# A two-layer decoder trunk: norm scales spread by two float32r products, and narrower scores for the first query blocks

## The chip, the cores and the metric

The kernel runs on one core of a Trainium2 chip. A core has TensorE (PE in the rows; its weight loads stand apart as PEld), VectorE (DVE), ScalarE (ACT), GpSimd (POOL) and the DMA queues, here all issued from SyncE (SP). The metric is device time in microseconds for one execution, the median of several runs; less is better.

## What is computed

The input is 512 tokens of 1024 features in float32. Two layers follow, each with a token mixer and a gated MLP; every sub-layer has an RMS norm ahead of it and is added to the residual, and a last norm ends the trunk. Layer 0 mixes tokens by causal means over windows of 2, 4, 8 and 16; layer 1 is attention with 16 heads on 4 key-value heads, over a sliding window of 128 keys, with a sink for each head and a linear bias over distance.

```python
def rms_norm(x, g):
    y = xf * lax.rsqrt(jnp.mean(xf * xf, axis=-1, keepdims=True) + RMS_EPS)
    return (y * g).astype(x.dtype)

# attention, for each block of 128 queries: the keys of its own and of the previous block
scores = jnp.einsum('bnqkgd,bnskd->bnkgqs', q, kb) * (HEAD_DIM ** -0.5)
mask = ((dist >= 0) & (dist < WINDOW))[None] & (key_pos >= 0)[:, None, :]
scores = jnp.where(mask, scores + bias, -jnp.inf)
p = jnp.exp(scores - m)
probs = p / (jnp.sum(p, axis=-1, keepdims=True) + jnp.exp(sink - m))
o = jnp.einsum('bnkgqs,bnskd->bnqkgd', probs, vb)

# MLP
u = h @ w_in                     # 1024 -> 2 x 2816
c = causal_depthwise_conv(u, width 3) + conv_b
h = h + (a * silu(g)) @ w_out    # a, g: the halves of c

for i in range(DEPTH):           # DEPTH = 2
    h = h + mixer_i(rms_norm(h, norm_mix[i]))
    h = h + conv_glu_ffn(rms_norm(h, norm_ffn[i]), ...)
return rms_norm(h, norm_f)
```

The first query block (b = 0) has no previous block, so only 128 of its 256 key columns are ever valid.

## The kernel before

Activations lie with features on the partitions: eight tiles `h` of 128 features by 512 tokens. Nearly all the work is matrix products. Every float32 operand of them is split into a high part in float32r (a rounding by an ACT copy, names ending in h) and the rest (a DVE or POOL subtraction, names ending in l), and `mm3` (L82 to L86) makes three products of them: high by high (L84), weight-high by low (L85), weight-low by high (L86). In the rows a product's operands stand as out<-moving,stationary or in the other order, and float32r tiles that PE reads are printed as f32. Weights come by `fetch` from SP's queue, three raw tiles deep, and are split by `weights` (L93 to L102).

PSUM has eight banks, handed out in rings by name. In the MLP six banks form the ring of the projections (`ps`), two the ring `aux`.

A norm (class `Norm`) is applied late. `stats` (L233 to L240) sums the squares over the features by products of `n_acc` with two columns of `ones`, and gives `n_r`, 128 tokens on the partitions by 4 token tiles. The scale is needed along the free dimension, the same on all partitions, so `spread` (L242 to L252) makes for each token tile the diagonal matrix `n_d` of the scales (DVE, L247) and multiplies it by the full matrix of ones in f32 (L248, two records in the trace for each product); ACT copies the bank to `n_rb` (L251). `spread` is called four times: in the first half of the MLP of layer 0 (two groups of products behind the statistics), in the attention (behind the query projection 2, and ahead of the products with `wv`), in the MLP of layer 1, and for the first 256 tokens at the end. In the MLP the products of the first groups run before the scale is known: four banks wait for `n_rb`, which the first step of the conv (L365) multiplies them with.

In the attention there are 16 units (n, b), a group n of four heads that share keys by a block b of 128 queries. For a unit, `scores` (L593 to L630) makes eight products (L609) of 256 moving columns, a high and a low part of the keys for each of four heads; a query tile `q` holds a head in one half of the partitions and the rest of its splitting in the other. DVE adds the bias and finds the largest (L612), ACT takes the exponential (L625), POOL divides (L629). For b = 0 these read 128 columns only: `w` is 128 there and 256 elsewhere. `transposed` turns the result on PE (L637), ACT and DVE split it (`th` L640, `tl` L641), and `weighted` multiplies it by the values; ACT and DVE split that into `oh` and `ol` (L656, L657). The steps of units 4, 2 and 0 places back are put together, and pieces of the query projections (`fill_q`) and of the output projection (`fill_wo`) are put between them at a fixed rate, so that PE has work while the other engines do the softmax. `queries` makes a new query tile from a bank: DVE scales (L513), ACT rounds (L520), DVE subtracts (L521), for two tiles.

The code gives each engine's instructions in program order, and a scheduler of the tile framework, which has its own durations for each instruction, moves them before the program is built, except for those held by `pin`. So a change in one place moves instructions in others.

Of the kernel before, what the change touches and what calls it, by code (L numbers as in the profile page):

```python
# [19 lines left out]
F32 = mybir.dt.float32  # L20
F32R = mybir.dt.float32r
I32 = mybir.dt.int32
AF = mybir.ActivationFunctionType
ALU = mybir.AluOpType
AX = mybir.AxisListType

P = 128
D = 1024
S = 512
# [28 lines left out]
def trunk(ctx: ExitStack, tc: tile.TileContext, x_tok, x_t, vecs, w_pool, w_kq, w_v, w_o, w_in, w_out, out_a, out_b):  # L58
    nc = tc.nc
    V, A, G, T = nc.vector, nc.scalar, nc.gpsimd, nc.tensor  # L60
    PSUM = bass.MemoryType.PSUM

    cst = ctx.enter_context(tc.tile_pool(name="cst", bufs=1))
    wp = ctx.enter_context(tc.tile_pool(name="wp", bufs=4))
    xp = ctx.enter_context(tc.tile_pool(name="xp", bufs=NC))
    sm = ctx.enter_context(tc.tile_pool(name="sm", bufs=2))


    def small(pool, n, words, dt=F32, **kw):
        return pool.tile([P, words], dt, **kw)[:, :n]  # L70
# [6 lines left out]
    def bank(tag):  # L77
        rings[tag].append(rings[tag].pop(0))
        return banks[rings[tag][-1]]
# [77 lines left out]
    ident = cst.tile([P, P], F32, name="ident")  # L157
# [11 lines left out]
    for g, w in enumerate(WINDOWS):  # L169
# [5 lines left out]
        f = band[:, 4 + g, : w - 1]  # L175
# [3 lines left out]
            edge_copy(g)  # L179
    ones = cst.tile([P, P], F32, name="ones")  # L180
    G.memset(ones, 1.0)


    def rsqrt_mean(dst, ssq, n, root=False):
# [28 lines left out]
    class Norm:  # L213
# [27 lines left out]

        def spread(self, ps, r, tiles=range(NT)):  # L242

            dg = sm.tile([P, S], F32, tag="sq", name=f"{self.name}_d")
            for i, j in enumerate(tiles):
                sl = slice(j * P, (j + 1) * P)
                V.tensor_scalar(dg[:, sl], ident, r[:, i : i + 1], None, ALU.mult)  # L247
                T.matmul(ps[:, sl], lhsT=ones, rhs=dg[:, sl], start=True, stop=True)  # L248
            rb = sm.tile([P, S], F32, tag="rb", name=f"{self.name}_rb", bufs=1)
            lo, hi = tiles[0] * P, (tiles[-1] + 1) * P  # L250
            A.activation(rb[:, lo:hi], ps[:, lo:hi], AF.Copy)  # L251
            return rb  # L252

# [183 lines left out]
    with tc.tile_pool(name="ap", bufs=2) as ap:  # L437
# [40 lines left out]
        r = norm1.stats(bank("av"))  # L478
# [51 lines left out]
        for j in range(NT):  # L530
            ps = vps[j // 2][:, (j % 2) * 256 : (j % 2 + 1) * 256]
            vv = ap.tile([P, 256], F32, tag="vv", name=f"vv{j}", bufs=1)
            V.scalar_tensor_tensor(vv, ps, r[:, j : j + 1], vec[:, V_BV : V_BV + 256], ALU.mult, ALU.add)
            dh, dl = (t[:, j, : 8 * HD].rearrange("p (n z d) -> p n z d", n=4, z=2)[:, :, 1, :] for t in (vh, vl))
# [58 lines left out]
        def scores(n, b):  # L593
            w = P if b == 0 else 2 * P
            neg = small(ap, 4, 32, tag="neg", name=f"neg{n}{b}", bufs=3)
            den = small(ap, 4, 16, tag="den", name=f"den{n}{b}", bufs=3)
            sink = nsink[:, 4 * n : 4 * n + 4]
            kk = max(b - 1, 0) * P
            sc = []
            for pr in range(2):  # L600
                ps = bank("s")

                st = ap.tile([P, 2, 2 * P + 32], F32, tag="sc", name=f"sc{n}{b}{pr}", bufs=6)
                G.tensor_copy(st[:, :, w], sink[:, 2 * pr : 2 * pr + 2])
                for par in range(2):
                    o = ps[:, par * 256 : par * 256 + 256]
                    qt = q[2 * n + pr][par][:, b * P : (b + 1) * P]
                    for x, kt in enumerate(key[n]):
                        T.matmul(o, lhsT=qt, rhs=kt[:, kk : kk + 256], start=x == 0, stop=x == 1)  # L609
                for par in range(2):  # L610
                    i = 2 * pr + par
                    V.tensor_tensor_reduce(  # L612
                        out=st[:, par, :w],
                        in0=ps[:, par * 256 : par * 256 + w],
                        in1=dist[:, 2 * P - w :],
                        scale=-slopes[4 * n + i],
                        scalar=sink[:, i : i + 1],
                        op0=ALU.add,
                        op1=ALU.min,
                        accum_out=neg[:, i : i + 1],  # L620
                    )
                sc.append(st)
            for i in range(4):
                t = sc[i // 2][:, i % 2, : w + 1]
                A.activation(t, t, AF.Exp, bias=neg[:, i : i + 1], scale=-1.0, accum_out=den[:, i : i + 1])  # L625
            V.reciprocal(den, den)
            for i in range(4):
                t = sc[i // 2][:, i % 2, :w]
                G.tensor_scalar(t, t, den[:, i : i + 1], 1.0, ALU.mult, ALU.mult)  # L629
            return sc  # L630
# [32 lines left out]
        for i in range(NU + 4):  # L663
            base = AHEAD + i * RATE
            have = max(i - 4, 0)
            if i < NU:
                n, b = units[i]
                if b == 0:
                    fill(2 * n * NC, 0)
                sc[i] = scores(n, b)  # L670
                if b == 2 and n + 1 < NKV:
                    key[n + 1] = keys(n + 1)
            fill(base + 2 * RATE / 3, have)
            if 0 <= i - 4 < NU:
                weighted(*units[i - 4], pt.pop(i - 4))
            if 0 <= i - 2 < NU:
                pt[i - 2] = transposed(*units[i - 2], sc.pop(i - 2))
            fill(base + RATE, have)
# [11 lines left out]
    with tc.tile_pool(name="fp1", bufs=2) as fp:  # L690
# [33 lines left out]
        w = {m: (kept_weights if m == NB else out_weights)(1, 1, m) for m in range(NB, NC)}  # L724
# [5 lines left out]
        for m in range(NB, NC):  # L730
# [3 lines left out]
            elif m == NB + 1:  # L734
                rb = norm3.spread(bank("aux"), ra, range(2))
                turn(NB)
                for c in range(NC):
                    o = fp.tile([P, HS], F32, tag="o", name=f"o{c}", bufs=4)
# [5 lines left out]
        sq = norm3.square(NC - 1, HS, S)  # L744
        scale_chunk(NC - 1, HS, S)
        ps = bank("aux")
        for x, t in enumerate((norm3.acc, sq)):
            for j in range(2):
                T.matmul(
                    ps[:, 2 * j : 2 * j + 2],  # L750
                    lhsT=t[:, HS + j * P : HS + (j + 1) * P],
                    rhs=ones[:, :2],
                    start=x == 0 and j == 0,
                    stop=x == 1,
# [3 lines left out]
        r = small(sm, NT, 32, tag="r", name="n3b_r")  # L758
        for j in range(2):
            rsqrt_mean(r[:, j : j + 1], ps[:, 2 * j : 2 * j + 1], 1, root=True)  # L760
        for j in range(2):
            for a in range(2):
                o = fp.tile([P, S], F32, tag="ob", name=f"ob{j}{a}", bufs=4)
# [67 lines left out]
```

## Time and profile before

| | us |
|---|---|
| median of 3 runs | 924.77 |
| lowest and highest | 924.59, 926.54 |
| the profiled execution | 924.49 |
| its span, first to last instruction | 922.8 |
| PE busy, products | 912.7 |
| DVE busy | 574.1 |
| ACT busy | 421.2 |
| POOL busy | 128.8 |

Rows below come from the profiled execution, whose times start at the span's beginning. A row of the timeline has the start, the time from the start to the end of the row, the engine, the line, the operation, out<-in, the shape, and how many alike are put together; brackets hold how long the engine stood idle before and what ended it. The granted clock of PE is at its upper level in all of the span (mean 0.999).

### The profile page before, as it was taken

What the parts mean: (1) busy time and instruction counts of PE and PEld (TensorE: products, weight loads), DVE (VectorE), ACT (ScalarE), POOL (GpSimd) and SP (SyncE); (2) the same over time, 40 slices, a digit from 0 to 9 for tenths busy, and PEclk for the clock granted to TensorE, in tenths of its full rate; (3) what the DMA queues carried; (4) which work ended last, traced back from release to release, by engine and by line L of the source; (5) the groups of instructions that cost most, each with busy time, mean ns of one, the idle gap of its engine ahead of it and who ended that gap; (6) DMA issues with size and microseconds to landing.
All of it is one profiled execution on the core that took longest, in us unless ns stands there. A gap on an engine that the chain in (4) does not pass through costs nothing.

```text
span 922.8 us, 11710 instructions
## 1 busy us (share of the span) xinstructions
PE 912.7 (99%) x4419; PEld 769.1 (83%) x4419; DVE 574.1 (62%) x958; ACT 421.2 (46%) x666; POOL 128.8 (14%) x232
## 2 busy tenths in 40 slices
PE   8999999999999999999999999999999999999997
PEld 7888888888888888898888888888888888888896
DVE  7589766335777654455787472987743377677423
ACT  7654443223444443436887441644422244444532
POOL 3800000000000001226665040000000000000022
PEclk9999999999999999999999999999999999999999
DMA  8233322333223223322110041142233423222312
GB/s 334 70 114 114 110 68 80 94 129 114 92 92 101 70 80 101 129 92 92 47 47 24 27 137 68 67 160 85 65 93 100 137 91 101 105 77 64 95 61 92
DMA packets 28855, 88.13 MB, mean 96 GB/s; under 512 B 3200, under 2 KB 4352, under 8 KB 28800
## 3 DMA queue, kind: packets, MB, share of 16 engines
q1 hardware_dynamic: 28800, 87.40, 28.9%
q8 instruction: 34, 0.56, 0.2%
q14 instruction: 21, 0.17, 0.1%
HBM read 85.29 MB, written 2.10 MB: 95 GB/s over the span
## 4 chain that ended last, share of the span: by engine, by line
PE 91%; POOL 2%; issue 2%; ACT 1%; DMA 1%; DVE 1%; SPq 0%; ACTq 0%; POOLq 0%; DVEq 0%
PE bank L84 29%; PE bank L85 29%; PE bank L86 29%; POOL wi_l L101 2%; PE bank L609 1%; DMA wi_raw<-w_in 1%; PE bank L637 1%; POOL n_acc L231 1%; ACT sc L625 1%; PE bank L248 0%; DVE wi_l L101 0%; PE bank L237 0%; ACT q L520 0%; ACT wo_h L98 0%; SPq L145 0%
## 5 line engine op out<-in xcount | busy, mean ns | idle before, releaser
L98 ACT ACTIVATE wi_h<-wi_raw 128x1024 fp32r<-128x1024 f32 x88 | 93.2, 1062 | 102.2 <-PE bank L85 97.7
L84 PE MATMUL bank<-f0x_h,wi_h 128*128 128x512 f32 x352 | 137.1, 390 | 0.0
L84 PE MATMUL bank<-f1x_h,wi_h 128*128 128x512 f32 x352 | 137.1, 390 | 0.0
L84 PE MATMUL bank<-zh,wo_h 128*128 128x512 f32 (+1 forms) x363 | 137.1, 378 | 0.0
L86 PE MATMUL bank<-f0x_h,wi_l 128*128 128x512 f32 x352 | 137.0, 389 | 0.0
L86 PE MATMUL bank<-f1x_h,wi_l 128*128 128x512 f32 x352 | 136.9, 389 | 0.0
L85 PE MATMUL bank<-f1x_l,wi_h 128*128 128x512 f32 x352 | 136.9, 389 | 0.0
L85 PE MATMUL bank<-f0x_l,wi_h 128*128 128x512 f32 x352 | 136.9, 389 | 0.0
L86 PE MATMUL bank<-zh,wo_l 128*128 128x512 f32 (+1 forms) x363 | 136.6, 376 | 0.0
L85 PE MATMUL bank<-zl,wo_h 128*128 128x512 f32 (+1 forms) x363 | 136.5, 376 | 0.0
L231 POOL TENSOR_TENSOR n_acc<-n_acc,n_sq 128x512 f32<-128x512 f32 (+1 forms) x28 | 37.2, 1328 | 708.6 <-ACT n_sq L222 701.8
L101 DVE TENSOR_TENSOR wi_l<-wi_raw,wi_h 128x1024 fp32r<-128x1024 f32 x84 | 103.6, 1236 | 50.0 <-ACT wi_h L98 48.0
L98 ACT ACTIVATE wo_h<-wo_raw 128x768 fp32r<-128x768 f32 (+1 forms) x70 | 57.6, 824 | 124.0 <-PE bank L85 112.0
L365 DVE TENSOR_TENSOR c_u<-bank,n_rb 128x512 f32<-128x512 f32 x88 | 60.0, 687 | 76.3 <-PE bank L86 76.3
L101 DVE TENSOR_TENSOR wo_l<-wo_raw,wo_h 128x768 fp32r<-128x768 f32 (+1 forms) x66 | 60.4, 915 | 54.5 <-ACT wo_h L98 54.3
L86 PEld LDWEIGHTS bank<-zh,wo_l 128*128 128x128 f32 x363 | 68.3, 188 | 12.5
L85 PEld LDWEIGHTS bank<-zl,wo_h 128*128 128x128 f32 x363 | 68.3, 188 | 12.4
L84 PEld LDWEIGHTS bank<-zh,wo_h 128*128 128x128 f32 x363 | 68.3, 188 | 12.3
L86 PEld LDWEIGHTS bank<-f0x_h,wi_l 128*128 128x128 f32 x352 | 66.1, 188 | 13.8
L86 PEld LDWEIGHTS bank<-f1x_h,wi_l 128*128 128x128 f32 x352 | 66.1, 188 | 13.8
L84 PEld LDWEIGHTS bank<-f1x_h,wi_h 128*128 128x128 f32 x352 | 66.1, 188 | 13.7
L84 PEld LDWEIGHTS bank<-f0x_h,wi_h 128*128 128x128 f32 x352 | 66.1, 188 | 13.7
(173 smaller groups left out, 1471.3 us busy)
## 6 DMA issues: line engine op xcount, KB each, us to landing
wi_raw<-w_in SPq DMA_DIRECT2D x88, 512.0 KB, 3.2
wo_raw<-w_out SPq DMA_DIRECT2D x31, 384.0 KB, 3.0
wo_raw<-w_out SPq DMA_DIRECT2D x31, 320.0 KB, 2.9
kq_raw<-w_kq SPq DMA_DIRECT2D x10, 512.0 KB, 3.2
wo_raw<-w_o SPq DMA_DIRECT2D x8, 512.0 KB, 3.2
xt<-x_tok SPq DMA_DIRECT2D x4, 512.0 KB, 5.1
h<-x_t SPq DMA_DIRECT2D x8, 256.0 KB, 8.4
wpool_raw<-w_pool SPq DMA_DIRECT2D x2, 512.0 KB, 7.9
```

What stands on the lines that cost most here:

```text
L84: T.matmul(ps, lhsT=wh, rhs=xh, start=start, stop=False, **kw)
L85: T.matmul(ps, lhsT=wh, rhs=xl, start=False, stop=False, **kw)
L86: T.matmul(ps, lhsT=wl, rhs=xh, start=False, stop=stop, **kw)
L98: pin(A.activation(h[:, :n], raw[:, :n], AF.Copy))
L101: (eng or V).tensor_tensor(l[:, o], raw[:, o], h[:, o].bitcast(F32), ALU.subtract)
L231: eng.tensor_tensor(self.acc[:, lo:hi], self.acc[:, lo:hi], sq[:, lo:hi], ALU.add)
L365: V.tensor_tensor(u, ps, rb, ALU.mult)
L609: T.matmul(o, lhsT=qt, rhs=kt[:, kk : kk + 256], start=x == 0, stop=x == 1)
L625: A.activation(t, t, AF.Exp, bias=neg[:, i : i + 1], scale=-1.0, accum_out=den[:, i : i + 1])
L637: T.transpose(ps[:, i * P : (i + 1) * P], sc[i // 2][:, i % 2, kb * P : (kb + 1) * P], ident)
```

## The change

`spread` makes two diagonals for each token tile, a rounded one in float32r on ACT (`n_dh`) and the rest on DVE (`n_dl`), and then multiplies all token tiles at once: one product of 512 columns with each diagonal tile, 256 columns in the last call, against a float32r copy of the ones, accumulated in the bank. In `scores` the moving side has `w` columns, so 128 for b = 0 and 256 for the others as before; 32 of the 128 products are narrower.

```diff
     G.memset(ones, 1.0)
+    ones_r = cst.tile([P, P], F32R, name="ones_r")
+    G.tensor_copy(ones_r, ones)
...
         def spread(self, ps, r, tiles=range(NT)):
-            dg = sm.tile([P, S], F32, tag="sq", name=f"{self.name}_d")
+            dh, dl = (sm.tile([P, S], F32R, tag="sq", name=f"{self.name}_d{x}") for x in "hl")
+            lo, hi = tiles[0] * P, (tiles[-1] + 1) * P
             for i, j in enumerate(tiles):
                 sl = slice(j * P, (j + 1) * P)
-                V.tensor_scalar(dg[:, sl], ident, r[:, i : i + 1], None, ALU.mult)
-                T.matmul(ps[:, sl], lhsT=ones, rhs=dg[:, sl], start=True, stop=True)
+                A.activation(dh[:, sl], ident, AF.Copy, scale=r[:, i : i + 1])
+                V.scalar_tensor_tensor(dl[:, sl], ident, r[:, i : i + 1], dh[:, sl].bitcast(F32), ALU.mult, ALU.subtract)
+            for x, d in enumerate((dh, dl)):
+                T.matmul(ps[:, lo:hi], lhsT=ones_r, rhs=d[:, lo:hi], start=x == 0, stop=x == 1)
             rb = sm.tile([P, S], F32, tag="rb", name=f"{self.name}_rb", bufs=1)
-            lo, hi = tiles[0] * P, (tiles[-1] + 1) * P
             A.activation(rb[:, lo:hi], ps[:, lo:hi], AF.Copy)
...
-                    o = ps[:, par * 256 : par * 256 + 256]
+                    o = ps[:, par * 256 : par * 256 + w]
...
-                        T.matmul(o, lhsT=qt, rhs=kt[:, kk : kk + 256], start=x == 0, stop=x == 1)
+                        T.matmul(o, lhsT=qt, rhs=kt[:, kk : kk + w], start=x == 0, stop=x == 1)
```

Lines after the change are two higher behind L181 and four higher behind L248. The scheduler moves instructions in three places that the prediction speaks of.

PE in the first half of the MLP of layer 0, where the scales are spread, the change with - and + (`wi_2_0` is the weight group behind the spread; a product that stands there four times is two records each in the trace):

```order
 L86 MATMUL bank_70<-f0x_h,wi_2_1_l 128x512
-L248 MATMUL bank_77<-n_d,ones 128x128 x4
 L84 MATMUL bank_71<-f0x_h,wi_2_0_h 128x512
+L253 MATMUL bank_77<-n_dh,ones_r 128x512
+L253 MATMUL bank_77<-n_dl,ones_r 128x512
 L85 MATMUL bank_71<-f0x_l,wi_2_0_h 128x512
```

The two new products have moved behind one product of the next group. In the attention the first of them stands behind the first product of `wv` and the second behind its second; in layer 1 the first stands behind one product of the next group and the second behind four more.

ACT in the attention, units of group 2 (`sc` and `neg` are the scores and the largest of them, `q_0` a query tile of the last group), before:

```order
L98 ACTIVATE wo_h<-wo_raw 128x1024
L625 ACTIVATE sc_3964,den_3963<-sc_3964,neg_3962 128x257 x2
L625 ACTIVATE sc_3972,den_3963<-sc_3972,neg_3962 128x257 x2
L520 ACTIVATE q_0_3993<-bank_75,bqs 64x512
L656 ACTIVATE oh<-bank_71 128x2x128
L640 ACTIVATE th_4020<-bank_76 128x512
```

The same place after:

```order
L629 ACTIVATE sc_3972,den_3971<-sc_3972,neg_3970 128x257 x2
L629 ACTIVATE sc_3980,den_3971<-sc_3980,neg_3970 128x257 x2
L98 ACTIVATE wo_h<-wo_raw 128x1024
L524 ACTIVATE q_0_4001<-bank_75,bqs 64x512
L660 ACTIVATE oh<-bank_71 128x2x128
L644 ACTIVATE th_4028<-bank_76 128x512
```

The splitting of an output weight has moved from ahead of the four exponentials to behind them, and ahead of the query tile, `oh` and `th`.

PE at the first unit of head group 3 (`q7_0` is half of the last query tile, `wo0` the first output weight), before:

```order
L609 MATMUL bank2_72<-kh3_4062,q6_1_3996 128x256
L609 MATMUL bank2_72<-kl3_4063,q6_1_3996 128x256
L84 MATMUL bank5_75<-oh_3361,wo0_h_4201 128x512
L85 MATMUL bank5_75<-ol_3362,wo0_h_4201 128x512
L86 MATMUL bank5_75<-oh_3361,wo0_l_4202 128x512
L84 MATMUL bank5_75<-oh_3361,wo0_h_4201 128x512
L85 MATMUL bank5_75<-ol_3362,wo0_h_4201 128x512
L86 MATMUL bank5_75<-oh_3361,wo0_l_4202 128x512
L609 MATMUL bank3_73<-kh3_4062,q7_0_4136 128x256
L609 MATMUL bank3_73<-kl3_4063,q7_0_4136 128x256
```

The same place after:

```order
L613 MATMUL bank2_72<-kh3_4070,q6_1_4004 128x128
L613 MATMUL bank2_72<-kl3_4071,q6_1_4004 128x128
L84 MATMUL bank5_75<-oh_3369,wo0_h_4209 128x512
L85 MATMUL bank5_75<-ol_3370,wo0_h_4209 128x512
L86 MATMUL bank5_75<-oh_3369,wo0_l_4210 128x512
L613 MATMUL bank3_73<-kh3_4070,q7_0_4144 128x128
L613 MATMUL bank3_73<-kl3_4071,q7_0_4144 128x128
```

Three of the six products of `wo0` have moved from ahead of the first read of `q7_0` to behind it. Behind them, the reads of its partner `q7_1` stand after four products of `weighted` now, and after six and a transpose before; on DVE the subtraction that ends `q7_1` has moved behind a second `tl`.

## Rows read from the trace of the kernel before

**Rows 1.** The page, busy time of each engine, its share and its instructions.

```profile
PE 912.7 (99%) x4419; PEld 769.1 (83%) x4419; DVE 574.1 (62%) x958; ACT 421.2 (46%) x666; POOL 128.8 (14%) x232
```

**Rows 2.** Waits of PE's weight loads: total us, times, longest us.

```profile
PEld bank L84 <- DVE ol L657: 1.3, 4, 0.5
PEld bank L609 <- DVE q L521: 0.9, 3, 0.6
```

**Rows 3.** Timeline of PE, scores between two projections: start and duration in us.

```profile
428.44 0.39 PE L86 MATMUL bank<-ax_h,kq_l 128*128 128x512 f32 x1
428.67 0.28 PE L609 MATMUL bank<-kh,q 128*128 128x256 f32 x1
...
429.62 0.40 PE L84 MATMUL bank<-ax_h,kq_h 128*128 128x512 f32 x1
```

**Rows 4.** Timeline of PE's weight loads, products with two moving columns.

```profile
398.96 0.86 PEld L237 LDWEIGHTS bank<-ones,n_acc 128*128 128x128 f32 x7
```

**Rows 5.** Timeline at the spread of layer 0, all engines.

```profile
54.62 0.39 PE L86 MATMUL bank<-f0x_h,wi_l 128*128 128x512 f32 x1
54.82 1.06 ACT L98 ACTIVATE wi_h<-wi_raw 128x1024 fp32r<-128x1024 f32 x1 [3.21 <-PE bank L85]
54.88 0.87 DVE L247 TENSOR_SCALAR n_d<-ident,n_r 128x128 f32<-128x128 f32 x4
...
55.22 1.16 PE L248 MATMUL bank<-n_d,ones 128*128 128x128 f32 x8 [0.21 <-DVE n_d L247]
...
56.45 0.39 PE L85 MATMUL bank<-f0x_l,wi_h 128*128 128x512 f32 x1
```

**Rows 6.** Groups by line and shape: busy us, mean ns, idle before.

```profile
L251 ACT ACTIVATE n_rb<-bank 128x512 f32<-128x512 f32 x3 | 1.8, 598 | 0.6 <-PE bank L248 0.5
...
L251 ACT ACTIVATE n_rb<-bank 128x256 f32<-128x256 f32 x1 | 0.4, 385 | 3.6 <-PE bank L248 3.6
...
L533 DVE SCALAR_TENSOR_TENSOR vv<-bank,n_r,vec 128x256 f32<-128x256 f32 x4 | 1.9, 484 | 2.0 <-PE bank L86 1.9
...
L629 POOL TENSOR_SCALAR sc<-sc,den 128x128 f32<-128x128 f32 x16 | 5.7, 374 | 4.5 <-DVE den L626 4.5
```

**Rows 7.** Timeline at the spread of the attention, all engines.

```profile
404.34 0.88 DVE L247 TENSOR_SCALAR n_d<-ident,n_r 128x128 f32<-128x128 f32 x4
...
405.36 1.05 PE L248 MATMUL bank<-n_d,ones 128*128 128x128 f32 x8
405.38 1.06 ACT L98 ACTIVATE kq_h<-kq_raw 128x1024 fp32r<-128x1024 f32 x1 [5.07 <-issue]
...
406.48 0.28 PE L86 MATMUL bank<-wv_h,ax_l 128*128 128x256 f32 x1
```

**Rows 8.** Timeline at the spread of layer 1, DVE and PE.

```profile
577.20 1.22 DVE L101 TENSOR_TENSOR wi_l<-wi_raw,wi_h 128x1024 fp32r<-128x1024 f32 x1
...
578.05 1.05 PE L248 MATMUL bank<-n_d,ones 128*128 128x128 f32 x8
```

**Rows 9.** Timeline of ACT, DVE and PE near the moved `wo_h`.

```profile
472.85 1.06 ACT L98 ACTIVATE wo_h<-wo_raw 128x1024 fp32r<-128x1024 f32 x1
474.29 0.52 ACT L625 ACTIVATE sc<-sc,neg 128x257 f32<-128x257 f32 x1 [0.38 <-DVE neg L612]
...
478.10 1.28 DVE L641 TENSOR_TENSOR tl<-bank,th 128x512 fp32r<-128x512 f32 x2
...
479.42 0.28 PE L85 MATMUL bank<-tl,vh 128*128 128x256 f32 x1
```

**Rows 10.** Timeline at the first unit of head group 3, DVE and weight loads.

```profile
487.87 0.74 DVE L521 SCALAR_TENSOR_TENSOR q<-bank,bqs,q 64x512 fp32r<-64x512 f32 x1
...
488.67 0.19 PEld L609 LDWEIGHTS bank<-kh,q 128*128 128x128 f32 x1 [0.59 <-DVE q L521]
```

**Rows 11.** Timeline at the start, POOL's last small step and its reader on DVE.

```profile
6.45 0.22 POOL L177 TENSOR_TENSOR band<-band,ident 128x15 f32<-128x15 f32 x1
...
7.16 0.52 DVE L297 TENSOR_SCALAR sband<-band,r 128x576 f32<-128x576 f32 x1
```

## The prediction

> **What bounds the kernel now.** I read the table of engines first: PE is busy for 912.7 of 922.8 us [rows 1], so the time is the sum of PE's products plus what PE waits. The waits of PE's weight loads come next: in the attention they are small and hang on DVE and ACT, 1.3 us in four waits for `ol` and 0.9 us in three for `q`, the longest 0.6 [rows 2]. So an edit counts in two ways: how long PE's own instructions take, and whether PE comes to an operand that DVE or ACT has not finished. Prices on PE are distances from start to start, since the printed durations of neighbours overlap: a product with 512 columns of float32r takes 0.23 us, and one with 256 takes 0.119 (eight from 428.67 to 429.62) [rows 3]. A record with two moving columns still costs (0.86 - 0.19)/6 = 0.112 [rows 4]: that is a floor, set by the weight load that each record brings. An f32 product of 128 columns is two records; eight such records and two products of 256 columns stand between 405.36 and 406.48 [rows 7], so (1.12 - 0.24)/8 = 0.11 a record and 0.222 a product.
>
> **The change part by part.**
>
> *The first spread (layer 0).* Before, PE ends its stream of L86 near 54.85, waits for `n_d`, runs eight records from 55.22 and comes to L85 at 56.45 [rows 5]. After, PE takes one L84 (0.23), then the product of `n_dh`, then that of `n_dl`. ACT makes `n_dh` from about 54.82, ahead of the `wi_h` that starts there before [rows 5]. By the two widths of `n_rb`, 0.598 and 0.385 [rows 6], an ACT copy of 128 columns takes 0.28, and I estimate four of them, each begun 0.09 before the last ends, at 0.85: ready at 55.67. DVE makes four `n_dl` from 55.13 on. The nearest rows are the old `n_d`, four in 0.87 [rows 5], and the three-operand form at 256 columns, 0.484 [rows 6]; I take 1.16 for four, with ends at 0.87 and 1.94. So `n_dl` is ready at 56.29, its product streams from about 56.49, and L85 comes at 56.72: **+0.27** (ends -0.15 and +0.9). The removed products give nothing here: PE waits for the diagonals instead. `n_rb` comes some 0.5 later. Four of the six banks wait for it, but PE still has a whole group of 24 products (5.4 us) in the sixth, so the conv chain has time.
>
> *The attention's spread.* `n_r` is there when `n_d` starts at 404.34, and ACT is idle until 405.38 [rows 7], so `n_dh` is ready near 405.2 and `n_dl` near 405.8. PE does L84 of `wv`, `n_dh` and L85 from 405.36 to 405.83, waits a little, streams `n_dl` near 406.0, and starts L86 at 406.24 instead of 406.48: **-0.24** (ends -0.45 and +0.3). Behind, `n_rb` still waits for ACT's `kq_h`, so its user sees nothing.
>
> *The spread in layer 1.* DVE runs `wi_l` ahead of `n_dl`: four `n_d` that ended before 577.20 began near 576.4; put 1.22 and 1.16 there instead, and `n_dl` is ready near 578.8 [rows 8]. PE's order puts five other products (1.1 us) and `n_dh` between 578.05 and the product of `n_dl`, near 579.4. No wait, so 0.89 of records become 0.45: **-0.44**. *The last spread:* four records at 0.112 become two products at 0.119, **-0.21**; it feeds only the first half of the output.
>
> *The cast of ones.* It stands on POOL ahead of the last small L177, which ends at 6.67, while its reader `sband` starts at 7.16 [rows 11]. The nearest POOL row of that size is 0.374 [rows 6], under the 0.49 of slack: **0** (0 to 0.1).
>
> *The scores.* 32 of the 128 products at L609 shrink from 256 to 128 moving columns. No row shows a float32r product that narrow. The bounds: the floor of 0.112 [rows 4] gives at most 32 x 0.007 = -0.2; if the rate of float32r fell to that of f32, 0.222, they would cost 32 x 0.103 = +3.3; and if the time simply went with the columns, 0.067, -1.7. I take the floor, because the two-column record already sits on it, and **-0.06** of it, since each group's end is a wait.
>
> *What the scheduler moved along with it.* The narrower products are planned differently, and some neighbours change places. (1) ACT near 473: `wo_h`, 1.06 us at 472.85, goes behind four exponentials. These start at 474.29 only because they wait for `neg` [rows 9], so they don't come sooner; `q`, `oh` and `th` come 0.96 later. DVE's two `tl` then start at 479.06 instead of 478.10 and end near 480.3, while PE reads the first at 479.42 and the second some 0.7 later [rows 9]: **+0.4** (0 to 0.96). (2) PE in head group 3: before, six products of `wo` stand ahead of the first read of the last query tile, and PE still waits 0.59 there, until DVE's L521, 487.87 to 488.61, is done [rows 10]. After, three stand there. Nothing on ACT or DVE makes that tile earlier, so three products (0.68) move from cover to wait: **+0.68**. The partner tile's L521 also stands behind one more `tl` (0.68 at most); PE has four products of AV before it, and I take **+0.17** (0 to 0.69). The next `th` and `tl` follow later: **+0.15**. The other shifts (POOL's weight pieces, the order of conv steps) lie where PE has full banks ahead: 0. SP issues its transfers in the order of before.
>
> **The sum:** 0.27 - 0.24 - 0.44 - 0.21 - 0.06 + 0.4 + 0.68 + 0.17 + 0.15 = **+0.7 us**. The profiled execution took 924.49, so 925.2; the median of the runs, 924.77, is 0.28 above it: **925.5**. A measurement of this kernel can tell about 0.2%, 1.85 us, from no change, so the forecast is no change.
>
> **The rivals.**
>
> *A. Narrow float32r products run at f32's rate (slower; the other side).* Price: the +3.3 above. For it: no row under 256 columns exists, and the 256-column product sits so near the floor that the rows can't say what happens below. Against it: nothing in the f32 rows says that a short stream changes the rate. With it, PE reaches the queries later, so waits shrink: of the moved cover in head group 3 only some 0.2 is left, and of the other waits [rows 2] (2.2 less that 0.59, so 1.6) I let half go, 0.8. 3.3 - 0.6 (spreads) + 0.4 + 0.2 - 0.8 = +2.5: **927.3**, with ends near 926.5 and 928.3. It decides from about 0.2 for a narrow product: 0.088 over the floor, times 32, is 2.8, less the 0.8 and the 0.8 that head group 3 gives back, so 1.2 over the forecast.
>
> *B. Narrow products go with their columns.* 32 x 0.052 = -1.7 in PE's work. PE then comes to each wait earlier, and about half is lost: 0.7 - 0.85 = -0.15, **924.6**; if nothing is lost, 923.8. Against it is the two-column record at 0.112 [rows 4], which shortens no further. The Trainium skill ("TensorE: Matmul & The Clock Gate", section "Back-to-back issue gap") speaks for it: it gives an isolated gap of N/2.4 + 2.5 ns, about 56 ns at 128 columns, and about 81 ns in a stream of loads and products. By 81 ns the scores would save about 32 x 0.038 = 1.2 us, an estimate from that page; rows 4 disagree with it for f32 weights, and for float32r no run here shows it.
>
> *C. The new order costs nothing.* DVE and ACT could have slack that I don't see, since each step moves when another does. Then the sum is 0.27 - 0.24 - 0.44 - 0.21 - 0.06 = -0.7: **924.1**. For it: PE's waits in the attention are short, and a wait that is opened is often taken from the next. Against it: the wait of 0.59 before the last query tile [rows 10] shows that this place has no slack already.
>
> **How the numbers follow.** Forecast 0.52, A 0.30, C 0.10, B 0.08. The range must leave out at most 2 in 10. Of A, what lies over 927.8 is about a third, 0.09; of C and B, with the low ends of the spreads, about 0.07 lies under 923.8. So 923.8 to 927.8. Faster by over 0.2% means under 922.9, which none of the cases reaches without several low ends together: 0.05. Slower by over 0.2% means over 926.6: nine tenths of A and a tenth of the forecast, where both late query tiles and the first spread take their high ends: 0.32. Same: 0.63.
>
> **What the changed profile would show.** The starts of the narrow scores tell first: eight in 0.9 us is the floor, 1.8 is A, 0.55 is B. Layer 0 should show PE idle for about a microsecond in all around the two new products, layer 1 none, and the distance between their neighbours shorter by 0.44. The wait of the last group's scores for `q` should grow from 0.59 to about 1.3; if it doesn't, C holds. The AV products near 480 should wait for `tl`. PE's total busy time hardly tells, since the waits and the products change by amounts of one size. What would make the forecast wrong: a rate below 256 columns other than the floor, or an `n_dl` on DVE much slower than 0.3 each, which would push the layer-0 and attention spreads up together.

## The result: 2.6 us slower, and where they lie

The changed kernel takes **927.6 us** (median of 8 runs, 926.8 to 928.1), the kernel before 925.02 in runs beside it: a ratio of 1.0024, 95% interval [1.0014, 1.0033]. That is slower by a little over what a measurement can tell, inside the range, and 2.1 us above the forecast. The profiled execution took 927.48, with a span of 925.7 (before: 924.49 and 922.8).

The page's table of engines after the change answers to [rows 1]. PE's busy time didn't move (912.7 before), though its instructions fell by 20. So the 2.9 us by which the span grew stand in PE's idle time: 12.9 us now (925.7 less 912.8), 10.1 before.

```profile
PE 912.8 (99%) x4399; PEld 768.0 (83%) x4399; DVE 575.1 (62%) x958; ACT 425.9 (46%) x680; POOL 128.9 (14%) x233
```

The waits of PE's weight loads in the attention, from 428 to 521 us (total us, times, longest us), answer to [rows 2]. The wait for `q` has grown from 0.9 to 2.4, that for `ol` from 1.3 to 2.5.

```profile
PEld bank L84 <- DVE ol L661: 2.5, 6, 0.8
PEld bank L613 <- DVE q L525: 2.4, 3, 1.6
```

To place a loss I compare the start of the same product of PE in two profiled executions, and take the growth of its lateness from one landmark to the next. The landmarks, in the kernel before: the first two-column record of layer 0 (48.46), that of the attention (398.96), the first score product (428.67), the first two-column record of layer 1 (571.66) and of the last norm (905.40), and the end (922.78). The first column is all that comes ahead of layer 0's statistics. us, negative is a gain:

| | to layer 0's statistics | layer 0 with its spread | attention's spread | rest of the attention | layer 1 with its spread | last spread |
|---|---|---|---|---|---|---|
| forecast | 0 | +0.27 | -0.24 | +1.34 | -0.44 | -0.21 |
| the change | +0.40 | +0.84 | -0.03 | **+2.25** | -0.46 | -0.11 |
| e1, spreads alone | +0.65 | +0.92 | -0.03 | -0.05 | -0.45 | -0.26 |
| e2, scores alone | +0.98 | +0.53 | 0.00 | +2.55 | +0.01 | -0.01 |
| e5, `wo_h` first | +0.51 | +0.52 | -0.04 | +1.30 | -0.45 | -0.11 |
| e9, order of before | +0.51 | +0.92 | -0.03 | -0.07 | -0.45 | -0.26 |
| e4, e1 with later spreads | +0.58 | -0.61 | -0.45 | -0.03 | -0.45 | -0.27 |

Layer 0 must be read with care: e2 changes nothing there and still shows 0.98 and 0.53. In that execution ACT took up the first `h` 0.9 us later, when it had landed (18.26, before 17.39). What belongs to the spread begins where the scales `n_r` are done. From there to the L85 behind the spread, the kernel before takes 1.68 (54.77 to 56.45 [rows 5]) and the changed kernel 2.15 (55.53 to 57.68, below): **+0.47**, and within 0.01 of it in e1, e3, e5, e6, e7, e9 and e11. The other 0.37 of the change's 0.84 lies ahead of `n_r`, as all of e2's 0.53 does, and is not the spread's. `n_r` in the kernel before:

```profile
54.61 0.16 DVE L211 SCALAR_TENSOR_TENSOR n_r<-rs_t,rs_y 128x4 f32<-128x4 f32 x1
```

**The narrow scores** answer the question between the forecast and rivals A and B. Timeline of PE after the change, the stretch that answers to [rows 3]:

```profile
429.64 0.39 PE L86 MATMUL bank<-ax_h,kq_l 128*128 128x512 f32 x1
429.87 0.22 PE L613 MATMUL bank<-kh,q 128*128 128x128 f32 x1
429.93 0.28 PE L613 MATMUL bank<-kl,q 128*128 128x128 f32 x1
...
430.60 0.28 PE L613 MATMUL bank<-kl,q 128*128 128x128 f32 x1
430.71 0.45 PE L84 MATMUL bank<-ax_h,kq_h 128*128 128x512 f32 x1
431.00 0.40 PE L85 MATMUL bank<-ax_l,kq_h 128*128 128x512 f32 x1
```

The eight narrow products start between 429.87 and 430.60; from the second to the last it is 0.67 in six steps, 0.112 each: the floor. The first step is only 0.06, so the group takes 0.84 where [rows 3] had 0.95, but the wide product behind it then takes 0.29 (430.71 to 431.00) instead of 0.23, and little is left of it.

**Layer 0's spread**, all engines, answers to [rows 5]:

```profile
55.24 0.39 PE L84 MATMUL bank<-f0x_h,wi_h 128*128 128x512 f32 x1
55.37 0.16 DVE L213 SCALAR_TENSOR_TENSOR n_r<-rs_t,rs_y 128x4 f32<-128x4 f32 x1
55.63 1.28 ACT L250 ACTIVATE n_dh<-ident,n_r 128x128 fp32r<-128x128 f32 x4 [3.25 <-DVE n_r L213]
56.14 1.15 DVE L251 SCALAR_TENSOR_TENSOR n_dl<-ident,n_r,n_dh 128x128 fp32r<-128x128 f32 x4 [0.61 <-ACT n_dh L250]
56.96 0.49 PE L253 MATMUL bank<-n_dh,ones_r 128*128 128x512 f32 x1 [1.33 <-ACT n_dh L250]
57.35 0.50 PE L253 MATMUL bank<-n_dl,ones_r 128*128 128x512 f32 x1
57.68 0.40 PE L85 MATMUL bank<-f0x_l,wi_h 128*128 128x512 f32 x1
```

PE stands idle for 1.33 ahead of the product of `n_dh`: four copies on ACT take 1.28, not the 0.85 I had estimated; the four `n_dl` on DVE take 1.15, as assumed. But it is `n_dl` that ends the spread's chain: the weight load of its product waits for the last `n_dl`, done at 57.29.

```profile
57.34 0.19 PEld L253 LDWEIGHTS bank<-n_dl,ones_r 128*128 128x128 f32 x1 [0.20 <-DVE n_dl L251]
```

The four `n_dl` start 0.51 after ACT does (55.63 to 56.14), once the first copy is done, where I had put 0.31 (54.82 to 55.13); that is the 0.20 by which the spread costs more than the forecast's 0.27. The groups by shape (busy us, mean ns of one) show the price of all 14 copies, beside rows of 512 columns with a scale per partition (the `vec` in `f0x_h` and `px_h`) and without one:

```profile
L250 ACT ACTIVATE n_dh<-ident,n_r 128x128 fp32r<-128x128 f32 x14 | 4.5, 391 | 9.4 <-DVE n_r L213 9.3
L255 ACT ACTIVATE n_rb<-bank 128x512 f32<-128x512 f32 x3 | 1.8, 601 | 0.8 <-PE bank L253 0.7
L262 ACT ACTIVATE f0x_h<-h,vec 128x512 fp32r<-128x512 f32 x8 | 5.3, 721 | 0.0
L262 ACT ACTIVATE px_h<-bank,vec 128x512 fp32r<-128x512 f32 x8 | 5.0, 683 | 1.5 <-PE bank L303 1.5
L316 ACT ACTIVATE wpool_h<-wpool_raw 128x512 fp32r<-128x512 f32 x4 | 2.3, 622 | 0.3 <-DMA wpool_raw<-w_pool 0.2
```

In layer 1 the two products stand among others with no wait named, and the gain of 0.46 is the forecast's:

```profile
581.73 0.39 PE L253 MATMUL bank<-n_dh,ones_r 128*128 128x512 f32 x1
...
582.86 0.39 PE L253 MATMUL bank<-n_dl,ones_r 128*128 128x512 f32 x1
```

**The rest of the attention** holds the loss, and five stretches split it. Lateness of PE's transposes that stand at 481, 486, 491, 504 and 512 us in the kernel before, as growth from one to the next, from the first score product to layer 1's statistics:

| | 428.67 to 481 | to 486 | to 491 | to 504 | to 512 | to 571.66 | sum |
|---|---|---|---|---|---|---|---|
| the change | +0.29 | +0.63 | +1.06 | +0.44 | +0.08 | -0.25 | +2.25 |
| e3, first read later | +0.28 | +0.65 | +1.06 | +0.43 | +0.05 | -0.21 | +2.26 |
| e5, `wo_h` first | +0.28 | 0.00 | +0.76 | +0.43 | +0.06 | -0.23 | +1.30 |
| e7, e5 and e6 | +0.27 | 0.00 | +0.64 | +0.35 | +0.12 | -0.22 | +1.16 |
| e12, e7 and `oh` first | +0.28 | 0.00 | +0.64 | -0.06 | +0.01 | +0.02 | +0.89 |
| e9, order of before | -0.05 | 0.00 | -0.01 | 0.00 | 0.00 | -0.01 | -0.07 |

### The profile page after: what moved, and what is told of

Same layout as the page of the kernel before. It is cut to its first block, busy times and chain, and to the rows that moved or that the text cites. A ratio compares the mean times of both kernels' runs of the same rounds, so it can differ in the third digit from the quotient of the medians.

```text
span 925.7 us, 11683 instructions
## 1 busy us (share of the span) xinstructions
PE 912.8 (99%) x4399; PEld 768.0 (83%) x4399; DVE 575.1 (62%) x958; ACT 425.9 (46%) x680; POOL 128.9 (14%) x233
## 4 chain that ended last, share of the span: by engine, by line
PE 87%; ACT 3%; POOL 3%; issue 3%; DVE 2%; DMA 1%; SPq 0%; ACTq 0%; POOLq 0%; DVEq 0%
PE bank L84 28%; PE bank L86 28%; PE bank L85 28%; ACT sc L629 2%; POOL wi_l L101 2%; DMA wi_raw<-w_in 1%; POOL n_acc L233 1%; POOL sc L633 1%; PE bank L613 0%; PE bank L641 0%; DVE wi_l L101 0%; DVE tl L645 0%; ACT q L524 0%; ACT th L644 0%; POOL wo_l L101 0%
## 5 line engine op out<-in xcount | busy, mean ns | idle before, releaser
L85 PE MATMUL bank<-f0x_l,wi_h 128*128 128x512 f32 x352 | 137.1, 389 | 0.0
L85 PE MATMUL bank<-f1x_l,wi_h 128*128 128x512 f32 x352 | 136.9, 389 | 0.0
L85 PE MATMUL bank<-zl,wo_h 128*128 128x512 f32 (+1 forms) x363 | 136.6, 376 | 0.0
L85 PEld LDWEIGHTS bank<-zl,wo_h 128*128 128x128 f32 x363 | 68.3, 188 | 12.4
L85 PEld LDWEIGHTS bank<-f0x_l,wi_h 128*128 128x128 f32 x352 | 66.1, 188 | 14.3 <-DVE f0x_l L263 0.6
L85 PEld LDWEIGHTS bank<-f1x_l,wi_h 128*128 128x128 f32 x352 | 66.1, 188 | 13.7
```

Source lines behind the costliest of these rows:

```text
L85: T.matmul(ps, lhsT=wh, rhs=xl, start=False, stop=False, **kw)
```

## The experiments

The ratios are to the kernel before, timed beside each; their intervals are about 0.0009 (0.8 us) to either side. A tie ("behind") is an order-only dependency: it takes no operation away and adds none.

**Which half of the change loses.** e1 is the changed kernel with 256 columns put back into the scores; e2 is the kernel before with only the narrower scores.

```
-                    o = ps[:, par * 256 : par * 256 + w]
+                    o = ps[:, par * 256 : par * 256 + 256]
-                        T.matmul(o, lhsT=qt, rhs=kt[:, kk : kk + w], start=x == 0, stop=x == 1)
+                        T.matmul(o, lhsT=qt, rhs=kt[:, kk : kk + 256], start=x == 0, stop=x == 1)
```

> The float32r spread alone; the first blocks' scores are 256 columns wide as before. Theory (read from the trace of the changed kernel): the spread costs +0.84 us in layer 0, because n_dh on ACT takes 1.28 for four and n_dl ends 1.9 behind n_r while PE has one product to do; it gives about 0 in the attention, -0.45 in layer 1 and -0.1 at the end, so +0.3 in all, about 925.3; the attention's order is that of before, so PE's lateness grows by less than 0.2 between 428 and 517 us. If the first h tile lands 0.7 us later here too, as in the changed kernel, +0.4 comes on top (925.7); if it lands as before, that lateness was chance. Rival: a spread that starts the attention later makes its waits grow too, so most of the 2.6 us stands here, 927.

> The narrow scores alone, with the f32 spread of before. Theory: a product of 128 columns costs the floor of 0.111 us, so the 32 narrow products save at most 0.2 us; the moved wo_h on ACT (0.95) and the three wo products behind the first read of the last query tile (0.68), with the smaller moves around them, cost 2.2 us within the attention: 927.2, with PE on time (within 0.1) until 428 us. Rival: the lateness comes from the spread or the start, so the attention costs less than 0.5 here and the time is 925.0 to 925.5.

e1: 925.21, ratio 0.9998 [0.9989, 1.0007]. e2: 927.36, 1.0028 [1.0017, 1.0039]. The spreads are worth nothing in sum; the scores carry the whole loss, 2.55 of it in the attention.

**Is it the width or the order?** e9 keeps the narrow scores, and ties the attention's instructions on ACT, DVE, POOL and PE to the order that e1 has there.

```
+        for engine in ORDER:
+            row = [traced[n] for n in (f"I-{k}" for k in engine) if n in traced]
+            for prev, ins in zip(row, row[1:]):
+                tc.add_manual_dep(
+                    ins,
+                    prev.name,
+                    mybir.DependencyInfo(mybir.DependencyClass.NoSync, mybir.DependencyReason.DATA),
+                    reason="order",
+                )
```

> The changed kernel with every instruction of ACT, DVE, POOL and PE in the attention held in the order that it has with wide scores (the kernel with the spread alone, 925.21); only the 32 products are narrower. Theory: the narrow products cost the floor and save at most 0.2 us, and all that they cost was in the order, so the attention takes what it took before, within 0.2, and the time is 925.0 to 925.3. Rival: a part of the 2.25 us comes from the narrow products themselves (PE comes early and the chain of ACT and DVE meets it differently), so the attention stays 0.5 to 1.2 longer: 925.7 to 926.4.

925.23, 1.0001 [0.9992, 1.001], and the attention's lateness falls from +2.25 to -0.07. In their traces e9 and e1 have the same sequence of instructions on each of the four engines there, and differ in the width alone. **The loss is the order**, not the products: the scheduler has planned the narrower products differently, and so placed others differently. The waits of PE's weight loads in e9, the same stretch, are those of [rows 2] again:

```profile
PEld bank L91 <- DVE ol L669: 1.3, 4, 0.5
PEld bank L621 <- DVE q L533: 1.0, 3, 0.6
```

**Do narrower products shorten at all?** e11 is e9 with 64 moving columns in the first blocks' scores, so half of the scores that are read there are left out.

```
-                        T.matmul(o, lhsT=qt, rhs=kt[:, kk : kk + w], start=x == 0, stop=x == 1)
+                        c = 64 if b == 0 else w
+                        T.matmul(o[:, :c], lhsT=qt, rhs=kt[:, kk : kk + c], start=x == 0, stop=x == 1)
```

> As the run with the order of before, but the 32 products of the first blocks have 64 moving columns, so half of the scores that are read are left out. Theory: the weight load sets the distance from product to product, 0.11 us again, and the time is that of 128 columns, within 0.2. Rival: the distance goes with the columns or with the square of something smaller (0.06 to 0.08), the scores take 1 us less, and where PE is not waiting the time falls by up to that.

924.81, 0.9995 [0.9986, 1.0004]: the same as e9 within the intervals. The timeline of PE in e11 steps by 0.11 as with 128 columns:

```profile
429.28 0.28 PE L622 MATMUL bank<-kl,q 128*128 128x64 f32 x1
429.39 0.28 PE L622 MATMUL bank<-kh,q 128*128 128x64 f32 x1
...
429.95 0.28 PE L622 MATMUL bank<-kl,q 128*128 128x64 f32 x1
430.06 0.48 PE L91 MATMUL bank<-ax_h,kq_h 128*128 128x512 f32 x1
```

With this rivals A (0.222) and B (0.067 at 128 columns) both fall. The figure of about 81 ns that the Trainium skill ("TensorE: Matmul & The Clock Gate", section "Back-to-back issue gap") gives at 128 columns is not met here: 112 ns at 128 columns, and the same at 64.

**Which move costs what.** e3 puts PE's first read of the last query tile behind six products of `wo`, as before; e6 also puts, on DVE, the second `tl` of unit (2, 1) behind the subtraction that ends the partner tile, as before.

```
+                if (m, k) == (0, 1):
+                    behind(marks["s", 3, 0, 1, 0, 0], last)     # e3, e6
+        behind(marks["tl", 2, 1, 1], marks["q", 7, 1])          # e6
```

> The changed kernel with one move undone on PE: the first two products that read the last query tile stand behind six products of wo0 again, not three; nothing else moves. Theory: the wait before that read falls from 1.60 to about 0.9 and PE is 0.6 to 0.7 us less late behind it; about 927.0. Rival: PE is as late anyway because ACT and DVE are late from the moved wo_h, so the 0.68 turns up in the next wait (the second query tile, or ol) and the time stays at 927.6.

> The changed kernel with the order at the last query tile undone on both engines: on PE six products of wo0 ahead of its first read again, on DVE the subtraction that ends its second half ahead of the second tl again. With the PE move alone undone the first wait fell by 0.69 and the second rose by 0.67. Theory: the order on DVE holds the second half back by one tl (0.6 to 0.7), so with both undone the two waits together fall from 1.92 to about 1.2 and the time to 926.9. Rival: the lateness of ACT from the moved wo_h sets this place, the 0.7 turns up at the next wait for ol, and the time stays at 927.6.

e3: 927.71, 1.0028 [1.0018, 1.0038]. e6: 927.0, 1.0020 [1.0011, 1.0029]. Neither is told apart from the changed kernel; in the attention e3 wins nothing and e6 0.11. The timeline of PE's weight loads after the change, and then in e3, shows why:

```profile
491.10 0.19 PEld L613 LDWEIGHTS bank<-kh,q 128*128 128x128 f32 x1 [1.60 <-DVE q L525]
493.54 0.19 PEld L613 LDWEIGHTS bank<-kh,q 128*128 128x128 f32 x1 [0.32 <-DVE q L525]
```

```profile
490.52 0.19 PEld L626 LDWEIGHTS bank<-kh,q 128*128 128x128 f32 x1 [0.91 <-DVE q L536]
492.95 0.19 PEld L626 LDWEIGHTS bank<-kh,q 128*128 128x128 f32 x1 [0.99 <-DVE q L536]
```

The first wait lost 0.69 and the second gained 0.67: the tie moved three products from the second read's cover to the first's. Both tiles are late on DVE, so the two reads need more cover together, not another share of it. Nothing follows for the whole from which of them has it.

e6 is a weaker test than its ties suggest. With them the scheduler also put the partner's reads on PE behind two products of AV instead of four, and a step of the scores on DVE ahead of the partner's subtraction. So e6 doesn't have the order of before at this place, nor do e7 and e12, which have the same ties.

e5 puts `wo_h` ahead of the four exponentials on ACT; e7 is e5 with the ties of e6.

```
-                wo_w[m] = weights(w_o[m], D, f"wo{m}", ...)
+                wo_w[m] = weights(w_o[m], D, f"wo{m}", ...,
+                                  pin=(lambda ins: behind(marks["e", 2, 1, 0], ins)) if m == 2 else (lambda ins: ins))
```

> The changed kernel with one move undone on ACT: the splitting of output weight 2 (wo_h) stands ahead of the four exponentials of unit (2, 1) again (POOL's pieces of that weight come back with it). Theory: the exponentials wait for neg anyway, so wo_h is free there, and q, oh, th and the next exponentials come 0.95 earlier; the wait for ol before the products of weighted near 486 us falls from 0.80 to about 0.2, and PE is 0.6 to 0.95 less late from there on: 926.7 to 927.0. Rival: the order on DVE and PE at the last query tile decides alone, PE is as late behind it as before, and the time stays at 927.6.

> The changed kernel with all three moves undone (wo_h on ACT, the products on PE, the subtraction on DVE). Theory: nearly all of what the narrow scores cost (927.36 for the narrow scores alone against 925.13) is in these moves, so 925.4 to 925.9, the rest being smaller moves near 445, 457 and 502 us. Rival: the narrow scores make the attention late in some other way (PE comes early to each wait, or exponentials come at other times), and the time stays above 926.5.

e5: 926.37, 1.0012 [1.0003, 1.0021]. e7: 926.06, 1.0010 [1.0002, 1.0019]. One instruction of 1.04 us put back on ACT, and with it the four subtractions on POOL that read it, returns 0.95 in the attention (2.25 to 1.30). ACT after the change, and then in e5:

```profile
477.77 1.04 ACT L98 ACTIVATE wo_h<-wo_raw 128x1024 fp32r<-128x1024 f32 x1
478.72 0.67 ACT L524 ACTIVATE q<-bank,bqs 64x512 fp32r<-64x512 f32 x1
...
483.22 0.51 ACT L629 ACTIVATE sc<-sc,neg 128x257 f32<-128x257 f32 x1 [1.90 <-POOL sc L608]
```

```profile
474.12 1.05 ACT L98 ACTIVATE wo_h<-wo_raw 128x1024 fp32r<-128x1024 f32 x1
475.56 0.51 ACT L641 ACTIVATE sc<-sc,neg 128x257 f32<-128x257 f32 x1 [0.39 <-DVE neg L628]
...
477.55 0.67 ACT L535 ACTIVATE q<-bank,bqs 64x512 fp32r<-64x512 f32 x1
...
482.05 0.51 ACT L641 ACTIVATE sc<-sc,neg 128x257 f32<-128x257 f32 x1 [1.90 <-DVE neg L628]
```

In e5 `wo_h` fills time in which ACT waits for `neg` anyway. After the change it stands between the exponentials and `q`. The idle time of ACT ahead of the next unit's exponentials is 1.90 in both kernels, so it absorbed none of the 1.04: ACT waits there for scores and DVE steps that are themselves late by as much.

e12 adds to e7 one more tie on ACT: at the first unit of head group 3, `oh` and the first `th` stand ahead of the second of the four exponentials, as before.

```
+                if i < NU and units[i] == (3, 0):
+                    behind(marks["e", 3, 0, 1], marks["th", *units[i - 2], 0])
```

> The kernel with wo_h ahead of the exponentials, and with the reads of the last query tile in the order of before (926.06), and beside it one more order-only tie: on ACT the second of the four exponentials at the first unit of head group 3 stands behind oh and the first th of the units before, as in the kernel before. If that move holds the remaining 1.16 us of the attention's lateness, as the idle 1.22 us of ACT ahead of the second exponential suggests, the attention's lateness falls to about 0.3 us and the time to about 925.2. If the wait for neg is only where an older lateness shows, the time stays at 926.0 and the attention's lateness at 1.1.

926.27, 1.0012 [1.0003, 1.0022]: not faster than e7, so the time speaks against my theory. (The profiled execution of e12 took 928.97, 2.7 over the median, at a granted clock of 0.995; 3.0 us of it were lost in layer 0, so only its attention is compared.) The trace is more divided: the stretch to 504 goes from +0.35 to -0.06, but in e7 0.22 was given back behind 512 that e12 doesn't get, and the 0.64 ahead of it is untouched. The tie also gave PE the order of before from 508 on, so the two aren't separated. The 0.64 sits where neither theory had put it, in the second read of the last query tiles. Weight loads of PE in e12:

```profile
492.94 0.19 PEld L627 LDWEIGHTS bank<-kh,q 128*128 128x128 f32 x1 [0.58 <-DVE q L536]
495.04 0.19 PEld L627 LDWEIGHTS bank<-kh,q 128*128 128x128 f32 x1 [0.89 <-DVE q L536]
```

The first wait is that of [rows 10] again (0.59). The second was 0.17 in the kernel before:

```profile
490.62 0.19 PEld L609 LDWEIGHTS bank<-kh,q 128*128 128x128 f32 x1 [0.17 <-DVE q L521]
```

There three products of `wo`, six of AV and a transpose stood between the two tiles' reads; now three of `wo` and two of AV do. The four products of AV and the transpose that are missing took 0.58 before (an estimate from their starts, 489.94 to 490.52), and by the step that now stands ahead of it DVE starts the partner's subtraction 0.16 later behind its last `tl` than before. Together that is 0.74, near the 0.72 by which the wait has grown. No run put either of them back by itself, so this is not shown.

**Spread products later.** e4 is e1 with the spread's two products moved back on PE: in layer 0 behind six products of the next group, in the attention behind twelve of `wv`. e10 is the same on e9, e8 on e7.

```
+                if layer == 0 and len(spreads) == 2 and k == 1:
+                    behind(spreads[0], last)
...
+                if (j, k) == (0, 3):
+                    behind(spreads[3], last)
```

> The float32r spread alone, as in the run with the spread alone, with its products put later on PE: in layer 0 behind six products of the next group instead of one, in the attention behind twelve of wv instead of one and two. Theory: the waits were for the diagonals alone, so layer 0 goes from +0.84 to about -0.2, the attention from 0 to -0.4, with -0.45 in layer 1 and -0.1 at the end: -1.1, about 923.9 (0.4 more if the first h tile lands late). Rival: the scales come about 1 us later to the conv steps, the banks come free later and PE waits for one, so that the time is that of the run with the spread alone or more.

> The same order of the attention, with the spread's products put later as in the run that took 923.37, and the narrow scores. Theory: 923.2 to 923.5, so the narrow scores are worth nothing that can be measured over 923.37. Rival: the narrow scores save their work in full now that no wait takes it (32 x 0.007 = 0.2, and 0.05 more each where a stream was longer than the load), 922.5 and less; or the repairs don't add up, as in the run that took 925.1.

> As the run before, and with the spread's products put later as in the run that took 923.37. Theory: the two repairs add up, 923.5 to 924.1; a narrow score at the floor gives nothing that can be measured over 923.37. Rival: the narrow products do save their 0.007 each (0.2 us) and PE's earlier arrival helps, 923.1; or the two repairs don't add up, 924.5 and more.

e4: **923.37**, 0.9981 [0.9973, 0.999]. e10: 923.58, 0.9982 [0.9973, 0.9991]. e8: 925.1, 1.0001 [0.9992, 1.001]. e4 and e10 beat both kernels. PE in e4 at the spread of layer 0 no longer stands idle:

```profile
56.56 0.39 PE L86 MATMUL bank<-f0x_h,wi_l 128*128 128x512 f32 x1
56.83 0.51 PE L264 MATMUL bank<-n_dh,ones_r 128*128 128x512 f32 x1
57.21 0.50 PE L264 MATMUL bank<-n_dl,ones_r 128*128 128x512 f32 x1
57.55 0.40 PE L84 MATMUL bank<-f0x_h,wi_h 128*128 128x512 f32 x1
```

But it isn't free of waits. The weight loads of the two products still wait 0.30 for `n_dh` and 0.20 for `n_dl` (1.75 and 0.20 after the change), and from 56.56 to 57.55 the three starts take 0.99 where three products at 0.23 would take 0.69. So about 0.3 is still lost there, an estimate, and in e8 and e10 PE itself stands idle for 0.35 and 0.33 ahead of `n_dh`.

The attention's spread went from -0.03 to -0.45 in all three, and layer 0 to -0.61 (e4) and -0.15 (e8, e10); counted from the end of `n_r` to the end of layer 0, it is -0.66 to -0.68 in all three, instead of +0.47. e8's time fell by 0.96 against e7, where e4's fell by 1.84 against e1 and e10's by 1.65 against e9. I had expected 923.5 to 924.1 for e8. Its interval begins at 924.5, so that was wrong, and the time is the one named for repairs that don't add up. The stretches don't say so: the two spreads win the same in e8 as in e4, and the rest of the attention is 1.21 late, as in e7 (1.16). The difference between 0.96 and the other two falls is about as large as the intervals, so its cause stays open.

## Where the prediction was right and where it was wrong

**Right.** The floor of 0.112 for a narrow product (0.112); `n_dl` at 1.16 for four (1.15); layer 1 at -0.44 (-0.46); nothing for the cast (the first `px` product starts 0.04 later after the change); and that the order which the scheduler moved is the main cost, with the loss in the attention.

**Right in part by luck: the range, and term (2).** The forecast was no change, by the bound of 0.2%; the result lies over that bound, in the outcome that had 0.32 and not in the one that had 0.63. It is inside the range because the upper end was set for rival A, whose mechanism didn't occur. Term (2), the two reads of the last query tiles, found the place and came near in size: 0.68 + 0.17 = 0.85 forecast, +0.76 measured with `wo_h` back in its place (e5, 486 to 491). Its working is not borne out. e3 undoes the move that I priced at 0.68 and wins nothing, since the two reads share one cover, so that what one gains the other loses. With both moves tied back (e7) 0.64 is still lost, at the partner tile, for which I had 0.17.

**Wrong: term (1).** `wo_h` on ACT was sized at +0.4 with ends at 0 and 0.96; it costs 0.95 (e5), the high end. I had followed one reader, the two `tl`, and read PE's slack at it. The sign that I named for that, AV products near 480 waiting for `tl`, didn't come: PE's lateness doesn't grow there. But `q`, `oh` and `th` come late too, and the lateness grows at the wait for `ol` (0.63, 481 to 486) and again at those for `q` (0.30). The first of these waits after the change, which neither the kernel before nor e5 has:

```profile
486.22 0.19 PEld L84 LDWEIGHTS bank<-th,vh 128*128 128x128 f32 x1 [0.80 <-DVE ol L661]
```

**Wrong, "the next `th` and `tl`" and "the other shifts".** +0.15 was forecast for what follows in group 3; the stretch to 504 lost 0.44, which the one tie of e12 removes. About half of that returns later without the tie, so the tie is worth 0.27 in the attention (1.16 to 0.89). And the moves around 466, which I put down at nothing, cost 0.29: PE's wait for `q` there is 0.48 in e7 and 0.17 before. This was not tried by itself; e9 undoes it along with all the others.

**Wrong, the copies.** An `n_dh` takes 0.391 and four take 1.28, where I had taken 0.28 and 0.85 from the two widths of `n_rb`. Those copies have no scale per partition; `hg`, the scaled copy ahead of the output, has one, and its two widths in the groups by shape of the kernel before put 128 columns at 0.40 (an estimate, along the line through both):

```profile
L708 ACT ACTIVATE hg<-h,vec 128x512 f32<-128x512 f32 x5 | 3.6, 723 | 0.8 <-DVE h L703 0.8
L708 ACT ACTIVATE hg<-h,vec 128x256 f32<-128x256 f32 x6 | 3.0, 506 | 12.3 <-DVE h L703 12.3
```

In layer 0 only the first copy counts, as shown above: with the hand-over from ACT to DVE, which I had put at 0.03, it makes the spread +0.47 instead of +0.27. In the attention PE waits for the last of the four, and that wait of 0.41 takes up nearly all of the gain (-0.03 instead of -0.24):

```profile
406.97 0.19 PEld L253 LDWEIGHTS bank<-n_dh,ones_r 128*128 128x128 f32 x1 [0.41 <-ACT n_dh L250]
```

In the profiled executions the change ends 2.88 late against the forecast's 0.7. Of the 2.2 between them 0.91 lie in the attention (2.25 for 1.34), 0.20 in layer 0's spread, 0.21 in the attention's spread and 0.10 in the last spread. The other 0.77 lie ahead of `n_r` in layer 0 (0.40 and 0.37), where e2 shows as much and more without a change. Rival A's time, 927.3, was met, but not its mechanism. Rival B falls; its 0.067 is no half of 0.119 (that is 0.060), which would have made its price 1.9 and not 1.7. Rival C falls: the new order does cost. The sign that I named for term (2), the wait for `q` from 0.59 to about 1.3, came as 1.60, and as 1.31 once `wo_h` was out of it.

## What to carry to other kernels

An edit that shortens an operation in a scheduler's plan is also an edit of the order: before it is credited, hold the old order and time it alone, since here the width was worth 0 and the order 2.3 us. Engines that feed each other in turn form a chain: here a step of 1.04 us put between two links of it cost 0.95, though its engine, ACT, was busy for only 46% of the span. Such a step belongs where that engine already waits for another. And when several small operations become one product that waits for all of them, move that product behind work that is ready.

## What the runs showed of the hardware

- A float32r product that brings its own weight load costs 0.112 us from start to start at 128 and at 64 moving columns, beside 0.119 at 256 and 0.23 at 512: below 256 columns only 0.007 a product is left to save.
- ACT's copy of 128 columns from `ident` with a scale per partition took 0.391. At 512 columns copies with such a scale took 0.721 (`f0x_h`, from `h`) and 0.683 (`px_h`, from a bank), and copies without one 0.622 (`wpool_h`, from a raw tile) and 0.601 (`n_rb`, from a bank). So the scale costs 0.08 to 0.10, and the source 0.02 to 0.04.
- Executions whose code is the same up to layer 0's statistics reached them between 0.06 us early (e7) and 1.27 late (e10); ACT took up the first `h` at 17.34 in the one and at 19.07, after a wait for its landing, in the other. A stage must be compared from its own beginning, and in more than one execution.
